# A transformer block of two feed-forwards and a hybrid attention on one core: another order of the seven products and of the filling matmuls

## The chip, the cores and the metric

The kernel runs on one core of a Trainium2 chip. The core has a matrix engine (TensorE, PE in the profile; its weight loads have a row of their own, PEld), VectorE (DVE), ScalarE (ACT), GpSimd (POOL) and SyncE (SP), which issues the DMAs here. The metric is the device time of one execution in microseconds (us); lower is better. Times are the median of several runs.

## The reference

One block in float32, 512 tokens of 1024 features, with a feed-forward on each side of a mixer and a norm at the end:

```
x = x + 0.5 * swiglu(rmsnorm(x, norm_ffn1), w_ffn1_gate, w_ffn1_up, w_ffn1_down)
x = x + hybrid_mixer(rmsnorm(x, norm_mix), w_in, ..., w_out, rel_bias)
x = x + 0.5 * swiglu(rmsnorm(x, norm_ffn2), w_ffn2_gate, w_ffn2_up, w_ffn2_down)
return rmsnorm(x, norm_final)

swiglu(h, w_gate, w_up, w_down) = (silu(h @ w_gate) * (h @ w_up)) @ w_down     # D_FF = 2816
```

The mixer projects to 16 heads of 64 features. Eight of them attend to chosen blocks of keys ("MoBA"). The other eight ("NSA", in two groups of keys) add three results, each with a gate of its own: attention to compressed keys, to selected blocks and to a window. With 512 tokens all blocks are within reach, so that both kinds come down to masked softmax attention with a bias by distance; the compressed keys and values come from a small network of their own. `w_out` projects the heads' outputs back.

## The kernel before, in words

**Three matmuls for one.** A float32 product is made as three products of rounded parts: each operand is split into `hi` (ACT copies it, rounded) and `lo` (DVE or POOL subtracts), and `mm3` (L92 to L95) multiplies hi by hi, hi by lo and lo by hi into one bank of PSUM. These three are called a **triple** here. A triple over 512 tokens has three matmuls of 512 columns, one over half the tokens three of 256.

**Feed-forwards.** A hidden block is 128 of the 2816 hidden features; there are 22. The first six are made plainly (`plain`, 512 columns). The other 16 go two at a time through `pair` (L279): gate and up of two blocks and two halves of the tokens are a 2 x 2 matrix product, made with seven products instead of eight (Strassen and Winograd). A product is 8 triples of 256 columns, 24 matmuls: two halves `m` (gate, up) of four triples over k. The sums of weights S1 to S4 are DVE's (L293), the halves `sph` and `spl` are ACT's and DVE's (L203, L204). The products go into three banks, u, v and w (`pu`, `pv`, `pw`), and some go into a bank that holds an earlier one. What the bank then holds is first copied (`copied`, `wc<-pu`), or else combined with a copy at once (`c11`, `c12`, `c22`, `c21`), before the next product may add to it.

The way down (`down`, L350) has 512-column triples into `pd`, one of two banks of tag `mm`; when an output row block d is complete, DVE adds it to x (`half_added`, L477). The way down of one group of hidden blocks is laid as **fills** between the products of the next group: `mixed` (L382) does it for four hidden blocks at once, that is for two pairs or 28 steps (two to a product). A group has 36 fills at first (six blocks, less twelve that come earlier), then three times 32. By weights, `mixed` puts them behind every second step, with a threefold share behind the last step of the fourth product, S2, which S3 follows into the same bank. So two to five triples stand in a row. `go` (L395) writes PE's order by hand; loads, sums and halves are called 26.0, 12.8 and 8.6 us ahead by the steps' planned costs, and what comes after a product (`then`) is called before the next fill or behind the next step. A scheduler orders the other engines.

**Attention** is a list of steps, each with logits (`ps_s`), a turn (transposes into `ps_t`, then `th` on ACT and `tl` on DVE) and values (`po`). The loop at L1112 takes values of step i - 9, the turn of step i - 6 and logits of step i, with fills between these three. An NSA pair of heads has 13 steps: even head three for each of two kinds, odd head three, then the pair's compressed attention (`cmp_pair`: logits `ps_c` with ten DVE instructions, turn `ps_ct`, values `po<-th,vc`, L1023), then three more. The compressed values come last into the even head's bank; behind them `out_halves` (L869) empties that bank with one instruction of ACT (L882) and two of DVE (L883, L884). Fills are triples of the projections still due (`pp`; DVE's `t`, ACT's and DVE's `xo`, and copies by SP follow when one is complete) and of `w_out` (`pw`). How many stand at a loop step is a table, `share`, in triples; a running target makes whole numbers of it:

```
            if i in busy:
                share[i] += 4.0
            if i + 1 in starts or i + 1 == len(steps):
                share[min(i + 9, len(share) - 1)] += 2.0
```

`busy` holds the steps of `cmp_pair`, `starts` the first step of each head.

Of the kernel before, what the change touches and what calls it, by code (L numbers as in the profile page):

```python
# [32 lines left out]
def block_kernel(ctx: ExitStack, tc: tile.TileContext, A: dict, out: bass.AP):  # L33
# [141 lines left out]
    class Ffn:  # L175
# [103 lines left out]
        def pair(self, f):  # L279
# [8 lines left out]
            def sums(name):  # L288

                a11, a12, a21, a22 = [A[i, j] for i in range(2) for j in range(2)]  # L290
                to, x, y, op = {"S1": (a21, a21, a22, ALU.add), "S2": (a11, a21, a11, ALU.add),
                                "S3": (a21, a11, a22, ALU.subtract), "S4": (a12, a11, a12, ALU.add)}[name]
                nc.vector.tensor_tensor(to, x, y, op)  # L293

            def halves_of(name):
                half[name] = self.split(A[{"A11": (0, 0), "A12": (0, 1), "S1": (1, 0), "S2": (0, 0), "S3": (1, 0),
                                           "S4": (0, 1), "A22": (1, 1)}[name]])

            def run(m, to, a, b, first):
                if first and m == 0:  # L300
                    bank[to] = ps.tile([128, 2, HT], F32, name="p" + to, tag={"u": "s", "v": "t", "w": "o"}[to],
                                       bufs=2)
                hi, lo = half[a]
                for k, x in enumerate(self.moving(b)):
                    mm3(bank[to][:, m], (hi[:, m, k], lo[:, m, k]), x, first and m == k == 0, k == 3, True)
# [29 lines left out]
            for n, (to, a, b, first, then) in enumerate((  # L335
                    ("u", "A11", "B11", True, lambda: copied("u", "u1")),
                    ("v", "A12", "B21", True, c11),
                    ("w", "S1", "T1", True, lambda: copied("w", "w1")),
                    ("u", "S2", "T2", False, lambda: copied("u", "u2")),
                    ("u", "S3", "T3", False, c22),  # L340
                    ("w", "S4", "B22", False, c12),
                    ("u", "A22", "T4", False, c21))):
                for m in range(2):
                    steps.append(Step(1.36, lambda m=m, to=to, a=a, b=b, first=first: run(m, to, a, b, first),
                                      (lambda n=n: loads(n)) if n < 2 and m == 0 else None,
                                      (lambda a=a: sums(a)) if a[0] == "S" and m == 0 else None,
                                      (lambda a=a: halves_of(a)) if m == 0 else None, then if m else None))
# [34 lines left out]
        def mixed(self, steps, fills):  # L382

            out, done = [], 0
            weight = [0 if i < 2 or i == len(steps) - 1 else 3 if i % 14 == 7 else 1 for i in range(len(steps))]
            for i, s in enumerate(steps):
                out.append(s)
                if i % 2 == 0 and i < len(steps) - 1:
                    continue
                upto = sum(weight[:i + 1]) * len(fills) // sum(weight)  # L390
                out += fills[done:upto]
                done = upto
            return out

        def go(self, steps):  # L395
# [4 lines left out]
            late = None  # L400
            with tc.manual_schedule(engines={mybir.EngineType.PE}):
                for i, s in enumerate(steps):
# [5 lines left out]
                    if not s.late and late:  # L408
# [5 lines left out]
                    if s.late:  # L414
# [64 lines left out]
    with ExitStack() as ph:  # L479
# [81 lines left out]
        pairs[18].post.append(put_rows)  # L561
        for i in range(8):
            pairs[26 + 3 * i].post.append(lambda i=i: copied_bias(i))
            pairs[54 + 6 * i].post.append(lambda i=i: copied_cmp(i))
# [3 lines left out]
    with ExitStack() as ph:  # L568
# [529 lines left out]
        for i in range(len(steps)):  # L1098
# [4 lines left out]
            if i + 1 in starts or i + 1 == len(steps):  # L1103
# [187 lines left out]
```

## Time and profile before

| | |
|---|---|
| median of 3 runs | 994.87 us (994.78 to 996.94) |
| the profiled execution's own time | 994.5 us |
| its span, first to last instruction | 992.7 us |
| granted clock of TensorE | 0.999 |
| feed-forward 1, pairs and way down | 75 to 359 us of the span |
| attention's steps | 436 to 620 us |
| feed-forward 2, pairs | 717 to 948 us |

The profile is of one execution. A row of the timeline has the start in us, the duration in us, engine, line, operation, tiles (output <- inputs) with their shapes, and a count; in brackets stands the idle time of the engine before it, and what ended it. Matmuls overlap: the next one starts long before the former one's row ends, so that the pace of PE is read from start to start. `L94` is line 94 of the kernel. Groups show a count, busy us, mean ns of one, and idle us before them with its cause.

### The profile page before, as it was taken

What the parts mean: (1) busy time and instruction counts of PE and PEld (TensorE: products, weight loads), DVE (VectorE), ACT (ScalarE), POOL (GpSimd) and SP (SyncE); (2) the same over time, 40 slices, a digit from 0 to 9 for tenths busy, and PEclk for the clock granted to TensorE, in tenths of its full rate; (3) what the DMA queues carried; (4) which work ended last, traced back from release to release, by engine and by line L of the source; (5) the groups of instructions that cost most, each with busy time, mean ns of one, the idle gap of its engine ahead of it and who ended that gap; (6) DMA issues with size and microseconds to landing.
All of it is one profiled execution on the core that took longest, in us unless ns stands there. A gap on an engine that the chain in (4) does not pass through costs nothing.

```text
span 992.7 us, 15609 instructions
## 1 busy us (share of the span) xinstructions
PE 978.9 (99%) x5944; PEld 867.7 (87%) x5944; DVE 705.4 (71%) x1118; ACT 499.3 (50%) x853; POOL 169.3 (17%) x297
## 2 busy tenths in 40 slices
PE   8999999999999999999999999999999999999997
PEld 6889989999999898888888888888899999999995
DVE  4996675877676475668788885688765778667743
ACT  7654343444444345577666674645443444334444
POOL 0000000000000044256655564800000000000002
PEclk9999999999999999999999999999999999999999
DMA  9633256332320135652323431643333322343002
GB/s 321 225 118 109 84 170 183 119 105 76 116 85 22 54 106 157 211 180 79 92 71 89 120 105 54 195 166 106 106 107 127 103 90 85 107 128 106 23 1 85
DMA packets 45742, 113.86 MB, mean 115 GB/s; under 512 B 10049, under 2 KB 14866, under 8 KB 45668
## 3 DMA queue, kind: packets, MB, share of 16 engines
q1 hardware_dynamic: 45380, 112.73, 36.7%
q8 instruction: 47, 0.77, 0.3%
q14 instruction: 27, 0.22, 0.1%
q10 hardware_dynamic: 288, 0.14, 0.1%
HBM read 100.08 MB, written 5.30 MB: 106 GB/s over the span
## 4 chain that ended last, share of the span: by engine, by line
PE 89%; DVE 2%; DMA 2%; POOL 2%; ACT 2%; SPq 1%; issue 1%; ACTq 0%; DVEq 0%; POOLq 0%
PE pd L93 8%; PE pd L94 8%; PE pd L95 8%; PE pu L95 6%; PE pu L93 6%; PE pu L94 6%; PE pgu L94 4%; PE pgu L95 4%; PE pgu L93 4%; PE pw L95 4%; PE pw L93 4%; PE pw L94 4%; PE ps_t L955 2%; PE pp L93 2%; PE pv L95 2%; PE pp L94 2%
## 5 line engine op out<-in xcount | busy, mean ns | idle before, releaser
L203 ACT ACTIVATE sph<-aw 128x1024 fp32r<-128x1024 f32 x114 | 120.9, 1060 | 229.9 <-PE pu L94 112.1
L204 DVE TENSOR_TENSOR spl<-aw,sph 128x1024 fp32r<-128x1024 f32 x114 | 139.3, 1222 | 56.4 <-ACT sph L203 56.3
L81 ACT ACTIVATE whi<-raw 128x1024 fp32r<-128x1024 f32 (+3 forms) x115 | 112.1, 977 | 103.3 <-PE pgu L94 24.6
L88 DVE TENSOR_TENSOR wlo<-raw,whi 128x1024 fp32r<-128x1024 f32 (+3 forms) x90 | 112.2, 1249 | 30.7 <-ACT whi L81 30.3
L93 PE MATMUL pd<-h,whi 128*128 128x512 f32 x320 | 125.8, 393 | 0.0
L94 PE MATMUL pd<-h,whi 128*128 128x512 f32 x320 | 125.8, 393 | 0.0
L95 PE MATMUL pd<-h,wlo 128*128 128x512 f32 x320 | 124.4, 389 | 0.0
L93 PE MATMUL pu<-th,sph 128*128 128x256 f32 x384 | 108.0, 281 | 0.0
L95 PE MATMUL pu<-th,spl 128*128 128x256 f32 x384 | 107.9, 281 | 0.0
L94 PE MATMUL pu<-tl,sph 128*128 128x256 f32 x384 | 107.8, 281 | 0.0
L293 DVE TENSOR_TENSOR aw<-aw 128x1024 f32<-128x1024 f32 x64 | 78.0, 1219 | 28.8 <-DMA aw<-in_wgu 28.8
L93 PE MATMUL pgu<-xo,whi 128*128 128x512 f32 x192 | 75.2, 391 | 0.9 <-ACT xo L129 0.9
L94 PE MATMUL pgu<-xo,whi 128*128 128x512 f32 x192 | 74.9, 390 | 0.6 <-DVE xo L130 0.6
L94 PEld LDWEIGHTS pu<-tl,sph 128*128 128x128 f32 x384 | 73.5, 191 | 1.8
L95 PE MATMUL pgu<-xo,wlo 128*128 128x512 f32 x192 | 74.7, 389 | 0.0
L93 PEld LDWEIGHTS pu<-th,sph 128*128 128x128 f32 x384 | 72.1, 188 | 2.0
L477 DVE SCALAR_TENSOR_TENSOR x<-pd,x 128x512 f32<-128x512 f32 x72 | 49.4, 687 | 33.7 <-PE pd L95 33.6
L86 POOL TENSOR_TENSOR wlo<-raw,whi 128x128 fp32r<-128x128 f32 x136 | 64.6, 508 | 50.4 <-ACT whi L81 50.4
L95 PEld LDWEIGHTS pu<-th,spl 128*128 128x128 f32 x384 | 72.1, 188 | 0.0
L93 PE MATMUL pw<-xo,sph 128*128 128x256 f32 x256 | 72.0, 281 | 0.0
L95 PE MATMUL pw<-xo,spl 128*128 128x256 f32 x256 | 71.9, 281 | 0.0
L94 PE MATMUL pw<-xo,sph 128*128 128x256 f32 x256 | 71.9, 281 | 0.0
(253 smaller groups left out, 2437.8 us busy)
## 6 DMA issues: line engine op xcount, KB each, us to landing
aw<-in_wgu SPq DMA_DIRECT2D x64, 512.0 KB, 3.8
raw<-in_wgu SPq DMA_DIRECT2D x23, 512.0 KB, 5.5
raw<-in_wd SPq DMA_DIRECT2D x22, 512.0 KB, 3.6
raw<-in_wd2a SPq DMA_DIRECT2D x18, 512.0 KB, 3.8
raw<-in_w_a SPq DMA_DIRECT2D x16, 512.0 KB, 3.7
raw<-in_w SPq DMA_DIRECT2D x8, 512.0 KB, 4.2
kvn<-xo SPq DMA_DIRECT2D x32, 128.0 KB, 2.4
aq<-xo SPq DMA_DIRECT2D x32, 128.0 KB, 2.7
```

The costliest lines, as they stand in the source:

```text
L81: nc.scalar.activation(hi[:, s], src[:, s], AF.Copy)
L86: nc.gpsimd.tensor_tensor(lo[:, i, b], src[:, i, b], f32(hi[:, i, b]), ALU.subtract)
L88: nc.vector.tensor_tensor(lo[:, s], src[:, s], f32(hi[:, s]), ALU.subtract)
L93: nc.tensor.matmul(p, w[0], v[0], start=first, stop=False, skip_group_check=again)
L94: nc.tensor.matmul(p, w[0], v[1], start=False, stop=False, skip_group_check=again)
L95: nc.tensor.matmul(p, w[1], v[0], start=False, stop=last, skip_group_check=again)
L203: nc.scalar.activation(hi, v, AF.Copy)
L204: nc.vector.tensor_tensor(lo, v, f32(hi), ALU.subtract)
L293: nc.vector.tensor_tensor(to, x, y, op)
L477: nc.vector.scalar_tensor_tensor(xs[d], p, 0.5, xs[d], ALU.mult, ALU.add)
L955: nc.tensor.transpose(p[:, wide:wide + 128], lps[qi][:, j * 128:(j + 1) * 128], ident)
```

## The change

**In both feed-forwards.** The seven products keep their operands and banks but stand in another order: u A11, v A12, **u S2, w S1**, u S3, w S4, u A22. No two products into one bank follow each other in it. The four sums are made two at a time, S1 and S2 ahead of S2's product, S4 and S3 ahead of S3's, and S3 is written over A11's place instead of A21's. A step is now half of what it was (two triples of k, planned at 0.67 and 0.69 us), so a group has 56 steps. `mixed` puts exactly one fill behind a chosen step: behind the second half-steps from the sixth step on, and, as there are more fills than those 25 places, behind evenly chosen first half-steps. No fill is left over behind a group. `go` tells a first half-step by its cost, and doesn't call a former product's `then` for a fill that stands inside a product. The steps at which the bias rows are written and copied have their numbers doubled.

**In attention** the two triples that stood at the ninth step behind the end of an even NSA head's own steps now stand at the ninth step behind `cmp_pair`'s, that is at the loop step of its values. Everything else in the table stays.

```diff
@@ -289,19 +289,21 @@
 
                 a11, a12, a21, a22 = [A[i, j] for i in range(2) for j in range(2)]
                 to, x, y, op = {"S1": (a21, a21, a22, ALU.add), "S2": (a11, a21, a11, ALU.add),
-                                "S3": (a21, a11, a22, ALU.subtract), "S4": (a12, a11, a12, ALU.add)}[name]
+                                "S3": (a11, a11, a22, ALU.subtract), "S4": (a12, a11, a12, ALU.add)}[name]
                 nc.vector.tensor_tensor(to, x, y, op)
 
+            two_sums = {"S2": ("S1", "S2"), "S3": ("S4", "S3")}
+
             def halves_of(name):
-                half[name] = self.split(A[{"A11": (0, 0), "A12": (0, 1), "S1": (1, 0), "S2": (0, 0), "S3": (1, 0),
+                half[name] = self.split(A[{"A11": (0, 0), "A12": (0, 1), "S1": (1, 0), "S2": (0, 0), "S3": (0, 0),
                                            "S4": (0, 1), "A22": (1, 1)}[name]])
 
-            def run(m, to, a, b, first):
-                if first and m == 0:
+            def run(m, n, to, a, b, first):
+                if first and m == n == 0:
                     bank[to] = ps.tile([128, 2, HT], F32, name="p" + to, tag={"u": "s", "v": "t", "w": "o"}[to],
                                        bufs=2)
                 hi, lo = half[a]
-                for k, x in enumerate(self.moving(b)):
+                for k, x in list(enumerate(self.moving(b)))[2 * n:2 * n + 2]:
                     mm3(bank[to][:, m], (hi[:, m, k], lo[:, m, k]), x, first and m == k == 0, k == 3, True)
 
             def copied(to, name):
@@ -335,16 +337,19 @@
             for n, (to, a, b, first, then) in enumerate((
                     ("u", "A11", "B11", True, lambda: copied("u", "u1")),
                     ("v", "A12", "B21", True, c11),
+                    ("u", "S2", "T2", False, lambda: copied("u", "u2")),
                     ("w", "S1", "T1", True, lambda: copied("w", "w1")),
-                    ("u", "S2", "T2", False, lambda: copied("u", "u2")),
                     ("u", "S3", "T3", False, c22),
                     ("w", "S4", "B22", False, c12),
                     ("u", "A22", "T4", False, c21))):
                 for m in range(2):
-                    steps.append(Step(1.36, lambda m=m, to=to, a=a, b=b, first=first: run(m, to, a, b, first),
-                                      (lambda n=n: loads(n)) if n < 2 and m == 0 else None,
-                                      (lambda a=a: sums(a)) if a[0] == "S" and m == 0 else None,
-                                      (lambda a=a: halves_of(a)) if m == 0 else None, then if m else None))
+                    for at in range(2):
+                        begins = m == at == 0
+                        steps.append(Step(
+                            (0.67, 0.69)[at], lambda m=m, at=at, to=to, a=a, b=b, first=first: run(m, at, to, a, b, first),
+                            (lambda n=n: loads(n)) if n < 2 and begins else None,
+                            (lambda a=a: [sums(s) for s in two_sums[a]]) if a in two_sums and begins else None,
+                            (lambda a=a: halves_of(a)) if begins else None, then if m == at == 1 else None))
             return steps
 
         def down(self, w, fs, then, tag="mm", group=1):
@@ -382,22 +387,22 @@
         def mixed(self, steps, fills):
 
             out, done = [], 0
-            weight = [0 if i < 2 or i == len(steps) - 1 else 3 if i % 14 == 7 else 1 for i in range(len(steps))]
+            ends, inner = range(5, len(steps) - 1, 2), range(6, len(steps) - 2, 2)
+            more = max(0, len(fills) - len(ends))
+            taken = set(ends[:len(fills)]) | {inner[(2 * n + 1) * len(inner) // (2 * more)] for n in range(more)}
             for i, s in enumerate(steps):
                 out.append(s)
-                if i % 2 == 0 and i < len(steps) - 1:
-                    continue
-                upto = sum(weight[:i + 1]) * len(fills) // sum(weight)
-                out += fills[done:upto]
-                done = upto
-            return out
+                if i in taken:
+                    out.append(fills[done])
+                    done += 1
+            return out + fills[done:]
 
         def go(self, steps):
 
             start, at = [0.0], [0, 0, 0]
             for s in steps:
                 start.append(start[-1] + s.cost)
-            late = None
+            late, inside = None, False
             with tc.manual_schedule(engines={mybir.EngineType.PE}):
                 for i, s in enumerate(steps):
                     for j, ahead in enumerate((26.0, 12.8, 8.6)):
@@ -405,13 +410,16 @@
                             if steps[at[j]].ahead[j]:
                                 steps[at[j]].ahead[j]()
                             at[j] += 1
-                    if not s.late and late:
+                    if not s.late and late and not inside:
                         late()
                         late = None
                     s.run()
                     for post in s.post:
                         post()
-                    if s.late:
+                    if s.cost < 0.68:
+                        inside = True
+                    elif s.late:
+                        inside = False
                         if late:
                             late()
                         late = s.then
@@ -558,10 +566,10 @@
                 fills = ffn.down(A["wd1"][f:], fs, half_added)
             else:
                 steps += ffn.down(A["wd1"][f:], fs, then, None, 4)
-        pairs[18].post.append(put_rows)
+        pairs[36].post.append(put_rows)
         for i in range(8):
-            pairs[26 + 3 * i].post.append(lambda i=i: copied_bias(i))
-            pairs[54 + 6 * i].post.append(lambda i=i: copied_cmp(i))
+            pairs[52 + 6 * i].post.append(lambda i=i: copied_bias(i))
+            pairs[108 + 12 * i].post.append(lambda i=i: copied_cmp(i))
         ffn.go(steps)
 
 
@@ -1100,7 +1108,10 @@
                 share[i] += 0.5
             if i in busy:
                 share[i] += 4.0
-            if i + 1 in starts or i + 1 == len(steps):
+                share[i + 9] += 2.0
+            elif starts.get(i + 1) in (9, 11, 13, 15):
+                continue
+            elif i + 1 in starts or i + 1 == len(steps):
                 share[min(i + 9, len(share) - 1)] += 2.0
             if starts.get(i) in (0, 2, 4):
                 share[i + 1] += 3.0
```

What becomes of it in the order of PE, first pair of feed-forward 1, between product A12 (`pv`) and the one behind it, before:

```order
L95 MATMUL pv_842<-xo_740,spl_776 128x256
L93 MATMUL pd_880<-h_410,whi_722 128x512
L94 MATMUL pd_880<-h_411,whi_722 128x512
L95 MATMUL pd_880<-h_410,wlo_723 128x512
L93 MATMUL pd_880<-h_461,whi_722 128x512
L94 MATMUL pd_880<-h_462,whi_722 128x512
L95 MATMUL pd_880<-h_461,wlo_723 128x512
L93 MATMUL pw_887<-xo_353,sph_801 128x256
```

After, inside product A12 (its m = 1):

```order
L95 MATMUL pv_842<-xo_740,spl_777 128x256
L93 MATMUL pd_863<-h_410,whi_722 128x512
L94 MATMUL pd_863<-h_411,whi_722 128x512
L95 MATMUL pd_863<-h_410,wlo_723 128x512
L93 MATMUL pv_842<-xo_355,sph_776 128x256
```

and behind the same product:

```order
L95 MATMUL pv_842<-xo_740,spl_777 128x256
L93 MATMUL pd_863<-h_461,whi_722 128x512
L94 MATMUL pd_863<-h_462,whi_722 128x512
L95 MATMUL pd_863<-h_461,wlo_723 128x512
L93 MATMUL pu_813<-th3_129,sph_801 128x256
L94 MATMUL pu_813<-tl3_130,sph_801 128x256
```

The two triples that stood in a row behind A12 are now one in the middle of its second half and one behind it, and S2 into `pu` follows it in place of S1 into `pw`. Over the whole of feed-forward 1 the order has 51 runs of fills before the final way down, now 132 (33 runs of two triples, 10 of three, 6 of four and 2 of five, and two triples more ahead of the final way down; now 132 of one). In feed-forward 2 it is 52 (one more run of two), now 132. The final way down of feed-forward 1 has 34 triples in a row with those two, now 32. Behind the last product of feed-forward 2 stand the 32 transposes `px` in one piece, where 13 of them stood ahead of its fifth product before.

PE in attention, where the second NSA pair's compressed values end its even head (`po_4804`), before:

```order
L926 MATMUL ps_s_5078<-kvn_3964,aq_4743 128x384
L1023 MATMUL po_4804<-th_5000,vc_4431 128x512
L1023 MATMUL po_4989<-th_5000,vc_4431 128x512
L955 MATMUL ps_t_5096<-ident_84,lpn_4903 128x128
L955 MATMUL ps_t_5096<-ident_84,lp_4927 128x128 x2
L93 MATMUL pp_5062<-xo_3361,whi_4640 128x512
L94 MATMUL pp_5062<-xo_3362,whi_4640 128x512
L95 MATMUL pp_5062<-xo_3361,wlo_4641 128x512
L925 MATMUL ps_s_5107<-kvn_3962,aq_4743 128x512
```

and after:

```order
L934 MATMUL ps_s_5042<-kvn_3964,aq_4743 128x384
L1031 MATMUL po_4804<-th_4994,vc_4431 128x512
L1031 MATMUL po_4983<-th_4994,vc_4431 128x512
L93 MATMUL pp_4837<-xo_3467,whi_4440 128x512
L94 MATMUL pp_4837<-xo_3468,whi_4440 128x512
L95 MATMUL pp_4837<-xo_3467,wlo_4441 128x512
L963 MATMUL ps_t_5063<-ident_84,lpn_4903 128x128
L963 MATMUL ps_t_5063<-ident_84,lp_4927 128x128 x2
L93 MATMUL pp_5100<-xo_3352,whi_4689 128x512
L94 MATMUL pp_5100<-xo_3353,whi_4689 128x512
L95 MATMUL pp_5100<-xo_3352,wlo_4690 128x512
L933 MATMUL ps_s_5104<-kvn_3962,aq_4743 128x512
```

One triple now stands between the values and the transposes and another behind the transposes. At the loop steps that are four earlier two triples less stand; the order of the three other pairs changes in the same way.

DVE there: the rows that belong to the end of a filling projection (`t<-pp`, `xo<-t`) stood among those of the steps ahead of the head's end. Before:

```order
L601 TENSOR_TENSOR t_5033<-pp_4837,R_100 128x512
L933 ISA lp_5004,m_4953<-ps_s_5003,tb_4740 128x512
L933 ISA m_4953 128x1
L1016 TENSOR_TENSOR th_5000<-ps_ct_4995,th_5000 64x512
L613 TENSOR_TENSOR xo_3508<-t_5033,xo_3507 128x512
L933 ISA lpn_5023,m_5028<-ps_s_5022,tb_4740 128x128
L933 ISA m_5028 128x1
L933 ISA lpn_5023,m_5028<-ps_s_5022,tb_4740 128x256
```

They now stand behind it, `t` behind the first of `out_halves`' two instructions (`to`) and `xo` four rows behind the second (`o51`):

```order
L891 TENSOR_TENSOR to_5056<-po_4804,o50_5054 64x512
L609 TENSOR_TENSOR t_5071<-pp_4837,R_100 128x512
L967 TENSOR_TENSOR tl_5013<-ps_t_5007,th_5012 128x512
L892 TENSOR_TENSOR o51_5055<-to_5056,po_4804 64x512
L948 RECIPROCAL m_5022<-m_5022 128x3
L941 ISA lp_5105,m_5022<-ps_s_5104,tb_4740 128x512
L941 ISA m_5022 128x1
L967 TENSOR_TENSOR tl_5068<-ps_t_5063,th_5067 128x384
L621 TENSOR_TENSOR xo_3508<-t_5071,xo_3507 128x512
```

## The prediction

> **What bounds the kernel.** I read the page first, then busy time by stage, then TensorE's (PE's) rows in order of time inside two stages.
>
> ```profile
> span 992.7 us, 15609 instructions
> PE 978.9 (99%) x5944; PEld 867.7 (87%) x5944; DVE 705.4 (71%) x1118; ACT 499.3 (50%) x853; POOL 169.3 (17%) x297
> ...
> 75.00:359.00 284.00, 284.00 (x1895) 260.82 (x1895) 195.82 (x222) 118.90 (x158) 8.84 (x9) 1.00 0.33 102
> 436.00:620.00 184.00, 180.35 (x1048) 153.47 (x1047) 144.09 (x415) 124.22 (x323) 108.35 (x219) 1.00 0.34 91
> 717.00:948.00 231.00, 231.00 (x1604) 215.24 (x1603) 161.92 (x181) 98.22 (x126) 0.00 (x0) 1.00 0.31 96
> ```
>
> Behind a stretch stand its length, the busy time of PE, weight loads, DVE, ACT and POOL, and the granted clock, DMA share and GB/s. PE is never idle in the two feed-forward stretches (284.00 of 284.00, 231.00 of 231.00), at a granted clock of 1.00. So nothing that another engine does sooner can shorten these; only the pace of PE's own instructions can. In attention (436 to 620) PE lacks 3.65 us. A busy PE can still go slower or faster, so I take the pace from start to start:
>
> ```profile
> 300.61 0.40 PE L93 MATMUL pd<-h,whi 128*128 128x512 f32 x1
> ...
> 301.99 0.28 PE L93 MATMUL pu<-xo,sph 128*128 128x256 f32 x1
> ...
> 304.00 0.28 PE L95 MATMUL pu<-xo,spl 128*128 128x256 f32 x1
> ```
>
> From 301.99 to 304.00 there are 17 steps between 256-wide matmuls: 0.118 us each. The two triples before them took 1.38 us.
>
> **FFNs: the pace of a triple.** The matmuls are the same in number and shape; only their neighbours change. So the term is what it costs PE to enter a run of 512-wide matmuls out of 256-wide ones:
>
> ```profile
> 96.62 0.40 PE L93 MATMUL pd<-h,whi 128*128 128x512 f32 x1
> ...
> 97.32 0.40 PE L93 MATMUL pd<-h,whi 128*128 128x512 f32 x1
> ...
> 100.05 0.28 PE L93 MATMUL pu<-th,sph 128*128 128x256 f32 x1
> ...
> 332.14 0.40 PE L93 MATMUL pd<-h,whi 128*128 128x512 f32 x1
> ...
> 355.29 0.39 PE L93 MATMUL pp<-xo,whi 128*128 128x512 f32 x1
> ```
>
> The last two rows bracket the final way down, 34 triples in a row: 23.15 / 34 = 0.681 us each. The run of five from 96.62 to 100.05 took 3.43, which is 0.025 more than 5 x 0.681. The first triple of the run took 0.70 (96.62 to 97.32); with rows that are rounded to 0.01 I take 0.697, so that 0.016 of the 0.025 falls on it and the rest on the second. A single triple between 256-wide matmuls stands in attention:
>
> ```profile
> 490.02 0.39 PE L93 MATMUL pp<-xo,whi 128*128 128x512 f32 x1
> ...
> 490.72 0.28 PE L99 MATMUL po<-th,kvn 128*128 128x256 f32 x1
> ```
>
> It took 0.70 as well. By the built programs' order, FFN 1 has 51 runs of two to five triples before the final one, and 132 single triples after; FFN 2 has 52 and 132. Each FFN therefore goes from about 51 x 0.025 = 1.3 us of entries to 132 x 0.016 = 2.1 us: **+0.8 each, +1.7 for both** with rounding upwards. Its bounds: nothing, if a single triple enters free; and 264 x 0.025 less 103 x 0.025, or +4.0, if a single one pays the whole entry.
>
> The Trainium skill (TensorE: Matmul & The Clock Gate, Back-to-back issue gap) gives a warm matmul N / 2.4 + 2.5 ns whatever stood before it, 216 ns for 512 columns and 109 for 256. By that rule the FFN term is zero; the rows here differ from it, with 0.681 / 3 = 0.227 us in a long run, more at its beginning, and 0.118.
>
> **FFNs: the other order.** What the new order takes away is the follow-up of two products into one bank: S3 went into bank u right after S2, whose copy ACT makes (the row `wc<-pu`).
>
> ```profile
> 285.81 0.28 PE L95 MATMUL pu<-th,spl 128*128 128x256 f32 x1
> ...
> 286.98 0.58 ACT L309 ACTIVATE wc<-pu 128x512 f32<-128x512 f32 x1
> ...
> 288.67 0.28 PE L93 MATMUL pu<-th,sph 128*128 128x256 f32 x1
> ```
>
> S2's last matmul starts at 285.81, the copy ends at 287.56 and S3 begins at 288.67: 1.1 us to spare, with four triples in between. So the old order cost no wait here and the new one saves none. Its cover is larger: the whole S1 product (24 x 0.118 = 2.8 us) plus its fills lies between S2 and S3, so I cost it at nothing. Without any cover it would cost the 1.75 from 285.81 to 287.56, in 16 pairs. DVE's four sums of a pair (S1 to S4) are now made two and two instead of one by one, at most one sum earlier or later than before, and planned 12.8 us ahead of their use; the loads belong to the same two products as before, so SP's queue has the same order there. The way down's bank is needed again soonest at one place of the first group: with 12 x 0.118 + 0.70 = 2.1 us of PE's work between the last triple of one output and the next triple into its bank, where it was 24 x 0.118 + 0.70 = 3.5. DVE's addition has to fit into that behind whatever DVE is at; I cost it at nothing, and at some tenths, once in each FFN, if it comes late.
>
> **Attention: where PE waits.** Here PE's idle time sits on the transposes:
>
> ```profile
> L955 PE MATMUL ps_t<-ident,lpn 128*128 128x128 f32 x144 | 27.8, 275 | 2.9 <-DVE tl L959 2.9
> ```
>
> Its five waits are these, each with the row that PE issued before it:
>
> ```profile
> 464.30 0.40 PE L95 MATMUL pp<-xo,wlo 128*128 128x512 f32 x1
> 464.86 0.30 PE L955 MATMUL ps_t<-ident,lpn 128*128 128x128 f32 x1 [0.16 <-DVE tl L959]
> ...
> 491.82 0.62 PE L1023 MATMUL po<-th,vc 128*128 128x512 f32 x2
> 493.74 0.30 PE L955 MATMUL ps_t<-ident,lpn 128*128 128x128 f32 x1 [1.29 <-DVE tl L959]
> ...
> 521.05 0.63 PE L1023 MATMUL po<-th,vc 128*128 128x512 f32 x2
> 522.58 0.30 PE L955 MATMUL ps_t<-ident,lpn 128*128 128x128 f32 x1 [0.90 <-DVE tl L959]
> ...
> 525.62 0.34 PE L100 MATMUL po<-tl,kvn 128*128 128x384 f32 x1
> 526.28 0.41 PE L955 MATMUL ps_t<-ident,lpn 128*128 128x128 f32 x2 [0.32 <-DVE tl L959]
> ...
> 552.53 0.40 PE L95 MATMUL pp<-xo,wlo 128*128 128x512 f32 x1
> 553.12 0.30 PE L955 MATMUL ps_t<-ident,lpn 128*128 128x128 f32 x1 [0.19 <-DVE tl L959]
> ```
>
> All five come at `po<-th,vc`, or one or two steps behind it, the compressed values that finish a pair's even head: the four places to which the change moves its two triples. Start to start, less 0.23 per 512-wide matmul (0.175 for 384): 0.33, 1.46, 1.07, 0.49, 0.36, together 3.7 us. The chain behind the longest one, on DVE and ACT:
>
> ```profile
> 486.34 0.56 DVE L933 CUSTOM_DVE_ANT_0 lpn<-ps_s,tb 128x384 f32<-128x384 f32 x1 [1.22 <-PE ps_s L926]
> ...
> 488.07 0.69 DVE L601 TENSOR_TENSOR t<-pp,R 128x512 f32<-128x512 f32 x1 [0.21 <-PE pp L95]
> ...
> 490.53 0.87 DVE L613 TENSOR_TENSOR xo<-t,xo 128x512 fp32r<-128x512 f32 x1
> ...
> 493.03 0.56 DVE L959 TENSOR_TENSOR tl<-ps_t,th 128x384 fp32r<-128x384 f32 x1 [0.34 <-ACT th L958]
> ...
> 487.83 1.06 ACT L81 ACTIVATE whi<-raw 128x1024 fp32r<-128x1024 f32 x1 [0.19 <-PE pp L94]
> ...
> 489.28 0.61 ACT L612 ACTIVATE xo<-t 128x512 fp32r<-128x512 f32 x1
> ```
>
> Before the head's end DVE still waits for PE (1.22 at 486.34), and has 0.34 of idle time left between `xo` at 490.53 and `tl` at 493.03; `xo` (0.87) stands in its way, and ACT has `whi` and `xo` in its. In the new order two triples less stand before, so DVE gets its scores sooner, and the fill's `t` and `xo` come behind `tl` in DVE's row. A triple (0.70) also stands between the values and the transposes. The weights and the copies that SP sends for a job (its queue is in order) move with the triples by the same two, and the heads that need them come later; I cost that at nothing. So 1.46 loses 0.70 to the triple and 0.87 to DVE: gone. 1.07 goes the same way. Of 0.49 I count half, since `t` (0.69) now stands before that `tl`, against 1.4 us of PE work. Of 0.33 and 0.36 I count half. Sum 1.46 + 1.07 + 0.25 + 0.35 = 3.1; I take off 0.2 for new tenths where the triples left: **-2.9**. What is late next is PE itself, since each triple moved is 0.70 of its own work. Bounds: all 3.7 gone; or nothing gained and the removed cover missed at its old place. No wait stands there now, so the nearest price is the longest of the five, and +1.5 is the other end.
>
> **Sum.** +1.7 - 2.9 = -1.2. The profiled execution took 994.5 us (span 992.7 and 1.8 around it), so 993.3; the median of the runs is 994.87, 0.4 above, so **993.7**.
>
> **Rivals.**
> - *PE leaves the slow pace of the 256-wide matmuls.* Once they go faster, behind transposes near the end:
>
> ```profile
> 949.70 0.28 PE L95 MATMUL pu<-th,spl 128*128 128x256 f32 x1
> ...
> 951.85 0.40 PE L93 MATMUL pd<-h,whi 128*128 128x512 f32 x1
> ```
>
>   19 steps in 2.15 us, 0.113 each. If a single triple leaves PE in that state, 2,688 products gain 0.0045 each, 12 us: about 982. Against it: after runs of two as of five the pace was 0.118 at once. 6%.
> - *The entry is free*: a matmul's pace doesn't depend on what stood before it. Then -2.9 alone, 992.0. Against it stand the 0.70 rows; for it, that they are only 0.016 above a long run's. 10%. This is what the formula of the Trainium skill above would give.
> - *Slower: every switch between widths costs more than the entry that I counted*, since the change also cuts products in the middle. The FFNs get 264 - 103 = 161 more interruptions. With the upper bound, 0.025 each, and no gain in attention the time is 994.9 + 4.0 = 998.9. It decides for slower from (3.0 + 2.9) / 161 = 0.037 us per interruption with attention's gain, or 0.019 without it. For it: 0.70 against 0.681 shows that PE settles only after some matmuls, and a product cut in two has to settle more often. 12%.
> - *The attention wait only moves*, because DVE has hardly a pause ahead of the head's end (0.34 behind `xo`) and behind it gets `t` and `xo` there: +1.7 alone, 996.6. 17%.
> - *The change does not do what it says*: the order shows single triples and the moved fills, so 0.
>
> **How the numbers follow.** The forecast as summed has 55%. A measurement of this kernel tells about 0.3% (3 us) from no change. Same: the forecast mostly, the moved wait, most of the free entry; 0.67. Faster: the fast pace, part of the free entry, the forecast's end where all 3.7 go and the FFN term is small; 0.19. Slower: 0.14. The range reaches from -3.7 with no entry cost (about 991.0) to most of the upper bounds (997.3); the two ends beyond, 982 and 998.9, are left out.
>
> **What would show it.** Triples in the FFNs at 0.69 to 0.70 start to start and 256-wide matmuls still at 0.118 would confirm the FFN term; 0.113 would make the forecast too high by up to 12 us, and a first matmul behind a triple well over 0.118 too low. In attention the idle time of `ps_t` should fall from 2.9 to under 1 us; new waits at the steps that lost their triples, or one step later on the same `tl`, would show that it only moved. Any idle time of PE inside the FFNs would refute that the new order is covered.

## The result, and the profile after

The changed kernel took **983.82 us** (median of 5 runs, 982.56 to 986.12) where the one before took 994.87: a ratio of 0.9888 with an interval of 0.9869 to 0.9906, or 9.4 to 13.0 us less. The forecast was 993.7, within 991.0 and 997.3. The direction was right, the size was not: the time lies near the 982 us of a rival that had been given 6%.

The page of the changed kernel, its first line and its line on the engines:

```profile
span 981.0 us, 15636 instructions
PE 970.0 (99%) x5944; PEld 857.6 (87%) x5944; DVE 702.2 (72%) x1118; ACT 499.0 (51%) x853; POOL 168.9 (17%) x297
```

As many matmuls, PE just as busy by its share, and a span 11.7 us shorter: PE's busy time fell by 8.9 us, since it worked faster, and its idle time by 2.8. Busy time by stretch says where. The kernel before, from the first product to the last matmul of the final way down in feed-forward 1, in attention (first logits to last values), and from feed-forward 2's first product to the end (columns as in the prediction):

```profile
82.54:355.06 272.52, 272.52 (x1842) 251.21 (x1841) 185.92 (x211) 111.69 (x147) 5.47 (x5) 1.00 0.34 103
433.30:614.40 181.10, 177.54 (x1039) 151.57 (x1038) 143.37 (x418) 124.05 (x320) 109.34 (x221) 1.00 0.34 92
710.89:992.70 281.81, 275.22 (x1869) 254.03 (x1867) 183.76 (x216) 120.27 (x169) 5.18 (x4) 1.00 0.28 88
```

and the same three in the changed kernel:

```profile
82.39:350.42 268.03, 268.03 (x1843) 245.47 (x1841) 185.03 (x211) 111.73 (x147) 5.48 (x5) 1.00 0.34 104
428.02:607.03 179.01, 176.75 (x1040) 151.78 (x1038) 142.67 (x418) 123.82 (x320) 109.35 (x222) 1.00 0.34 93
703.66:981.00 277.34, 270.72 (x1869) 248.45 (x1867) 182.86 (x216) 120.14 (x169) 5.18 (x4) 0.99 0.28 90
```

Feed-forward 1 lost 4.49 us and feed-forward 2 lost 4.47, PE without a pause in the first both times and at the same clock. Attention lost 2.09. The rest of the 11.7 is 0.64 between feed-forward 1 and attention, where one wait is gone, and small shifts.

PE's rows in the first pair after show the moment at which the pace changes. Ahead of the first fill, and behind it:

```profile
85.93 0.28 PE L93 MATMUL pv<-xo,sph 128*128 128x256 f32 x1
...
86.63 0.40 PE L93 MATMUL pd<-h,whi 128*128 128x512 f32 x1
...
87.33 0.28 PE L93 MATMUL pv<-xo,sph 128*128 128x256 f32 x1
...
88.58 0.28 PE L95 MATMUL pv<-xo,spl 128*128 128x256 f32 x1
```

From 85.93 to 86.63 there are 6 steps of 0.117 us, the pace of before. The triple takes 0.70. From 87.33 to 88.58 there are 11 steps of **0.1136** each, on the same engine, with the same operands, and that pace stays to the end of the stretch. So one triple put PE into the faster pace that the prediction had seen near the end of the kernel before.

In attention the groups of transposes and of compressed logits:

```profile
L963 PE MATMUL ps_t<-ident,lpn 128*128 128x128 f32 x144 | 27.9, 275 | 0.8 <-DVE tl L967 0.8
L1000 PE MATMUL ps_c<-kc,aq 128*128 128x64 f32 x32 | 4.1, 273 | 1.1 <-DVE t L611 1.0
```

The idle time of `ps_t` fell from 2.9 to 0.8 us, as forecast; 1.1 now stands at `ps_c`, behind DVE's `t` of a fill.

### The profile page after: what moved, and what is told of

It is laid out like the page before. It is cut to its first block, busy times and chain, and to the rows that moved or that the text cites. A ratio compares the mean times of both kernels' runs of the same rounds, so it can differ in the third digit from the quotient of the medians.

```text
span 981.0 us, 15636 instructions
## 1 busy us (share of the span) xinstructions
PE 970.0 (99%) x5944; PEld 857.6 (87%) x5944; DVE 702.2 (72%) x1118; ACT 499.0 (51%) x853; POOL 168.9 (17%) x297
## 4 chain that ended last, share of the span: by engine, by line
PE 93%; DMA 2%; POOL 1%; DVE 1%; issue 1%; SPq 1%; ACT 0%; DVEq 0%; ACTq 0%; POOLq 0%
PE pd L94 8%; PE pd L95 8%; PE pd L93 8%; PE pu L93 6%; PE pu L95 6%; PE pu L94 6%; PE pw L93 4%; PE pw L95 4%; PE pw L94 4%; PE pgu L94 4%; PE pgu L95 4%; PE pgu L93 4%; PE pv L93 3%; PE pv L95 3%; PE pv L94 3%; PE pp L93 3%
## 5 line engine op out<-in xcount | busy, mean ns | idle before, releaser
L95 PEld LDWEIGHTS pd<-h,wlo 128*128 128x128 f32 x320 | 60.1, 188 | 13.4
L93 PE MATMUL pw<-xo,sph 128*128 128x256 f32 x256 | 70.7, 276 | 0.0
L94 PE MATMUL pw<-xo,sph 128*128 128x256 f32 x256 | 70.7, 276 | 0.0
```

Source lines behind the costliest of these rows:

```text
L93: nc.tensor.matmul(p, w[0], v[0], start=first, stop=False, skip_group_check=again)
L94: nc.tensor.matmul(p, w[0], v[1], start=False, stop=False, skip_group_check=again)
L95: nc.tensor.matmul(p, w[1], v[0], start=False, stop=last, skip_group_check=again)
```

## The experiments

Eleven kernels and the changed one once more, each measured beside "before" on the same chip. "Stretch" below means feed-forward 1 from its first product to the last matmul of the final way down, and feed-forward 2 from its first product to the end: 272.52 and 281.81 us before, 268.03 and 277.34 after.

**The two parts alone.** The changed feed-forwards with the old table of attention, and the reverse:

```diff
-                share[i + 9] += 2.0
-            elif starts.get(i + 1) in (9, 11, 13, 15):
-                continue
-            elif i + 1 in starts or i + 1 == len(steps):
+            if i + 1 in starts or i + 1 == len(steps):
```

> The feed-forwards of after with the attention table of before. Read from the two traces, the feed-forwards' stretches are 4.5 us shorter each and attention 2.1 us. Theory (the parts are independent, the pace of the 256-wide matmuls pays for all of the feed-forwards): 994.9 - 9.0 = 985.9 us, pace 0.1133 from start to start in both. Rival (part of the gain comes from what attention leaves behind): 987 or more.

Measured: 986.59 us, ratio 0.9910 (0.9890 to 0.9931), about 9.0 us less; stretches 268.03 and 277.34, to 0.01 us those of after.

> The feed-forwards of before with the attention table of after. Theory (the moved fill is worth what the attention stretch shows): 994.9 - 2.1 = 992.8 us, transposes' idle time 2.9 down to about 1 us, a new wait of some 1.0 us at one ps_c. Rival (attention only got shorter because its inputs came earlier or PE was in another pace): 994.9 us. 256-wide matmuls stay at 0.118 in both feed-forwards.

Measured: 993.42 us, ratio 0.9977 (0.9966 to 0.9989), 1.1 to 3.4 us less; stretches 272.52 and 281.82, those of before. In its profile, of the slowest of its executions (995.76 us), the waits on `tl` at the compressed values are 0.33 to 0.37, as in after's, and the new wait at `ps_c` is 0.32; the whole group of `ps_t` still shows 2.8, not the expected 1, because PE waited 0.9 for POOL's `lpn` and 0.9 for another `tl` early in the attention. By the times, the parts add up, and the feed-forwards are four fifths of the whole.

**The order of the products, or the single fills?** After, with the products and their sums in the order of before:

```diff
...
-                    ("u", "S2", "T2", False, lambda: copied("u", "u2")),
                     ("w", "S1", "T1", True, lambda: copied("w", "w1")),
+                    ("u", "S2", "T2", False, lambda: copied("u", "u2")),
...
```

> After, but with the seven products (and the sums) in the order of before; fills stay single, at the same places. Theory A (the length of the run of 512-wide matmuls decides the pace): 0.113 us for 256-wide matmuls, as in after; S3 follows S2 into one bank with one triple between, so PE waits for the copy 1.75 - 0.70 = 1.05 us in each of 16 pairs: 983.8 + 16.8 = 1000.6 us. Theory B (the new order of the products makes the pace): 0.118 us, 1000.6 + 11.5 = 1012 us.

Measured: 1000.94 us, ratio 1.0059 (1.0041 to 1.0077). PE's rows at the first S3:

```profile
98.95 0.39 PE L95 MATMUL pd<-h,wlo 128*128 128x512 f32 x1
100.16 0.39 PE L93 MATMUL pu<-th,sph 128*128 128x256 f32 x1 [0.82 <-ACT wc L311]
```

ACT's row there, and then the group of these matmuls:

```profile
99.53 0.58 ACT L311 ACTIVATE wc<-pu 128x512 f32<-128x512 f32 x1
...
L93 PE MATMUL pu<-th,sph 128*128 128x256 f32 x384 | 107.8, 281 | 12.8 <-ACT wc L311 12.8
```

S3 starts when ACT's copy ends (100.11). From the last matmul ahead to S3 there are 1.21 us where 0.23 would do: 1.0 or a little more in 15 of the 16 pairs (in the last one, transposes stand between S2 and S3), and the first step of S3 then takes 0.22 where 0.113 is usual. The stretches are 277.12 and 285.70, 17.45 together above after's. But for the first five steps behind such a wait the 256-wide matmuls stay at 0.1133. So theory A: the order of the products doesn't make the pace. It makes room for the copy, without which single fills cost more than they bring.

**Two fills in a row, new order.**

```diff
...
+            n = (len(fills) + 1) // 2
+            taken = {ends[(2 * j + 1) * len(ends) // (2 * n)] for j in range(n)}
...
-                    out.append(fills[done])
-                    done += 1
+                    out += fills[done:done + 2]
+                    done += 2
...
```

> After, but with two fills in a row at half as many places (the ends of second half-steps), the products in the new order. Theory A (a run of one triple leaves PE in the fast pace, a run of two in the slow one): 256-wide matmuls at 0.118, 983.8 + 11.5 us for the pace, less 2 x (132 x 0.020 - 66 x 0.027) = 1.7 us of entries: 993.6 us. Theory B (the order of the products, or where the fills stand, decides): 0.113 stays, 983.8 - 1.7 = 982.1 us.

Measured: 994.33 us, ratio 0.9987 (0.9973 to 1.0001); nearly all of the gain is gone, near the 993.6 of theory A. Behind a run of two triples:

```profile
101.00 0.40 PE L93 MATMUL pd<-h,whi 128*128 128x512 f32 x1
...
101.69 0.28 PE L93 MATMUL pu<-th,sph 128*128 128x256 f32 x1
...
102.98 0.28 PE L95 MATMUL pu<-th,spl 128*128 128x256 f32 x1
```

Eleven steps in 1.29 us, 0.117 each, the slow pace at once. Stretches 273.22 and 282.27, slightly above those of before.

**From which length on?** Fills cut into single 512-wide matmuls, in runs of 1 to 9 in shuffled order:

```diff
...
+            ones = [(f, j) for f in fills for j in range(3)]
...
+                cycle = list(range(1, 10))
+                self.rng.shuffle(cycle)
+                sizes += cycle
...
```

> After, but the fills are cut into single 512-wide matmuls and laid in runs of 1 to 9 of them, in shuffled order, all at the ends of second half-steps, in both feed-forwards. Theory A1 (up to a whole triple leaves PE in the fast pace, from some length between 4 and 6 on it is left in the slow one, whatever the pace before): 256-wide matmuls stand at 0.113 behind runs of 3 and at 0.118 behind runs of 6 to 9, each in both orders; runs of 1 and 2 either make the pace 0.113 or leave it as it was. Theory A2 (what counts is that the run is one accumulation triple hi-hi, hi-lo, lo-hi, not its length): runs of 3 that are cut across triples fall out, as do 1 and 2. Theory A3 (only the state before counts and a long run resets it: three matmuls toggle the pace): 0.113 and 0.118 alternate.

One execution: 999.02 us, at a mean clock of 0.993, with two long pauses of PE inside runs; only its rows are used. Behind a run of four, then of three, and of five matmuls (rows with x2 hold two):

```profile
105.09 0.28 PE L93 MATMUL pw<-xo,sph 128*128 128x256 f32 x1
...
106.38 0.28 PE L95 MATMUL pw<-xo,spl 128*128 128x256 f32 x1
106.50 0.63 PE L374 MATMUL pd<-h,whi 128*128 128x512 f32 x2
106.97 0.40 PE L374 MATMUL pd<-h,wlo 128*128 128x512 f32 x1
107.20 0.28 PE L93 MATMUL pw<-xo,sph 128*128 128x256 f32 x1
...
107.99 0.28 PE L94 MATMUL pw<-xo,sph 128*128 128x256 f32 x1
...
181.50 0.28 PE L93 MATMUL pw<-xo,sph 128*128 128x256 f32 x1
...
182.40 0.28 PE L95 MATMUL pw<-xo,spl 128*128 128x256 f32 x1
```

After four: 11 steps in 1.29 (0.117). After three: 7 in 0.79 (0.113). After five, from the fourth matmul on: 8 in 0.90 (0.1125 from rounded rows). Over both feed-forwards, all runs of PE's rows that no wait disturbed, by the mean pace of the fifth to tenth 256-wide matmul behind each:

| 512-wide matmuls in a row | 1 | 2 | 3 | 4 | 5 | 6 | 7 | 8 | 9 |
|---|---|---|---|---|---|---|---|---|---|
| cases | 17 | 17 | 18 | 17 | 18 | 20 | 16 | 14 | 17 |
| pace behind, us | 0.113 | 0.113 | 0.113 | 0.118 | 0.113 | 0.118 | 0.118 | 0.118 | 0.118 |

No case differs from the others in its column, whether the pace ahead had been 0.113 or 0.118, and whichever matmul of a triple the run began with. A2 and A3 fall. A1 holds but for its one threshold: five is fast, though four is not. So in these feed-forwards PE's pace has two states, and the length of the last run of 512-wide matmuls sets which.

**All fills narrow.** The way down in 256-wide matmuls:

```diff
...
+                for s in (slice(0, HT), slice(HT, S)):
+                    mm3(bank[d][:, s], w, (v[0][:, s], v[1][:, s]), k == s.start == 0, k == n - 1, True)
...
```

> After, but every fill except one in each group of hidden blocks is made as six 256-wide matmuls (both halves of its 512 columns) in place of three 512-wide ones; the one that stays 512-wide is the second of its group. Theory (256-wide matmuls hold the pace of 0.1133 that a single triple sets, and the 0.020 us that each single triple pays above 0.680 goes): 256 x 0.020 = 5.1 us less than after, 983.8 - 5.1 = 978.7 us, six narrow ones at 0.680. Rival 1 (without single triples between them the 256-wide matmuls fall back to 0.118): up to 256 x 6 x 0.0045 + 11.5 = 18 us more, about 1002 us. Rival 2 (twice the weight loads, 256 x 3 = 768 more, cost something of their own): the six at more than 0.70, slower than 983.8 us.

Measured: 999.95 us, ratio 1.0047 (1.0030 to 1.0065). Behind the one 512-wide fill, then a narrow one, then a product:

```profile
89.74 0.28 PE L93 MATMUL pu<-th,sph 128*128 128x256 f32 x1
...
90.42 0.28 PE L93 MATMUL pd<-h,whi 128*128 128x256 f32 x1
...
91.14 0.28 PE L93 MATMUL pu<-th,sph 128*128 128x256 f32 x1
...
91.72 0.28 PE L95 MATMUL pu<-th,spl 128*128 128x256 f32 x1
```

Six steps in 0.68 (0.113), six narrow ones in 0.72 (0.120), then five in 0.58 (0.116 to 0.118). The time is near the 1002 of rival 1, and the sign of rival 2 is there too: six narrow matmuls took 0.72, over its 0.70 and over six at the slow pace. The narrow fill itself ends the fast pace. What in it does so was not found; their additional weight loads were not tested apart. It isn't the change of bank alone: in the next kernel products of 256-wide matmuls follow each other in different banks at 0.1133 (there `pu` ends and `pv` begins in the middle of such a stretch).

**Long runs with a single triple behind.** If the last run alone sets the state, a long run may stand, as long as a single triple follows soon:

```diff
...
+                taken[i], taken[i + 1] = n - 1, 1
...
```

> After, with the fills of each group laid as runs of seven triples behind second half-steps, each followed by one single triple behind the next half-step (six 256-wide matmuls later). Theory (a long run leaves the slow pace, the next single triple ends it): per eight triples 0.027 of entry for the long run, 6 x 0.0045 = 0.027 of slow pace and 0.020 for the single triple, 0.074 us in place of 8 x 0.020 = 0.160. Over eight groups of 32 to 36 triples that is 33 x 0.086 = 2.8 us less: 983.8 - 2.8 = 981.0 us. Rival (the slow pace stays until the end of a product or longer, as in e4_doubles): 994. Rival 2 (runs of 4.8 us without a product starve PE afterwards, waits on sph or aw): over 984 us.

Measured: 983.77 us, ratio 0.9895 (0.9882 to 0.9909): the time of after, not the 981.0 of the theory. PE's rows in the first group, at a wait in a run and then behind another run:

```profile
105.04 0.39 PE L95 MATMUL pd<-h,wlo 128*128 128x512 f32 x1
105.92 0.50 PE L93 MATMUL pd<-h,whi 128*128 128x512 f32 x1 [0.49 <-DVE x L490]
...
120.42 0.28 PE L93 MATMUL pu<-xo,sph 128*128 128x256 f32 x1
...
121.12 0.40 PE L93 MATMUL pd<-h,whi 128*128 128x512 f32 x1
...
121.82 0.28 PE L93 MATMUL pu<-xo,sph 128*128 128x256 f32 x1
...
122.39 0.28 PE L95 MATMUL pu<-xo,spl 128*128 128x256 f32 x1
```

Behind the long run 6 steps in 0.70 (0.117), behind the single triple 5 in 0.57 (0.114). That is the theory's mechanism, and the rival of 994 falls. But the stretches are only 0.49 and 0.46 shorter than after's, since a wait of 0.65 for a bank of the way down came up in each.

Then runs of fifteen and one:

> The same with runs of fifteen triples and one: 0.074 us per sixteen triples in place of 0.320; 16 x 0.246 + 2 of the remainders, about 4.0 us less than after: 979.8 us. Rival 2 (10 us of PE's work without a product, so that the weights of the way down come late or the products' engines pause): waits inside the feed-forwards, over 984 us.

Measured: 989.11 us, ratio 0.9947 (0.9934 to 0.9961): over rival 2's 984, and with a wait inside the feed-forwards. PE's rows in a run of fifteen, and DVE's there:

```profile
170.64 0.80 PE L93 MATMUL pd<-h,whi 128*128 128x512 f32 x1 [5.35 <-DVE x L490]
171.23 0.63 PE L94 MATMUL pd<-h,whi 128*128 128x512 f32 x1
...
174.64 0.63 PE L93 MATMUL pd<-h,whi 128*128 128x512 f32 x1
...
168.75 1.23 DVE L293 TENSOR_TENSOR aw<-aw 128x1024 f32<-128x1024 f32 x1 [8.00 <-DMA aw<-in_wgu]
169.90 1.28 DVE L490 SCALAR_TENSOR_TENSOR x<-pd,x 128x512 f32<-128x512 f32 x2
```

PE waited 5.35 us for a bank of the way down. The addition (`x<-pd,x`) that frees it stood on DVE behind a sum of weights, and that one waited 8.00 us for the load of `aw`. So it was the products' own weights that came late, not those of the way down. Behind the wait PE went at half its pace: from 171.23 to 174.64 the 8 steps take 0.426 each, at a granted clock of 0.51 (170.6 to 175.4).

Runs of seven and one in the later groups alone, and the changed kernel on the same chip:

> After, with its single fills in the first group of each feed-forward, where runs of seven made PE wait 0.65 us for a bank of the way down, and runs of seven triples and one in the other three groups. Theory (0.086 us less per eight triples and no wait): 24 x 0.086 = 2.1 us less than after in the same call. Rival (the lumps take as much in other places, as in e7_seven_and_one, whose whole time was that of after): no difference.

> The changed kernel itself, on the same chip as e11_lumps_later: 983.8 us, with the attention waits as in after.

Measured: 981.86 us (980.96 to 984.78) with runs only in the later groups, 982.08 (981.57 to 983.99) for the changed kernel itself. The stretches were 266.99 and 276.32, so 1.04 and 1.02 shorter: the 2.1 us are there. The whole time shows no difference between the two: runs of one kernel spread by 2 to 4 us here. The version is not shown to beat the changed kernel.

**Attention.** The two triples of each NSA pair at both places, then at neither:

> After, with two fill triples of each NSA pair at both places, the old one and the one behind the compressed values. Theory A (DVE's t and xo of a filling projection stand in the way of the turn's tl; the moved triples are cover too, about half and half): the waits on tl at the compressed values, 3.7 us before and 1.4 after, are 2 to 2.8 here. Theory B (the triple behind the values is cover, and nothing else counts): 1.4 as in after.

Measured: 986.37 us, ratio 0.9916 (0.9903 to 0.9930). The steps on `tl` at the compressed values, start to start less PE's own pace as in the prediction, are 0.33, 0.33, 0.34 and 0.72, together 1.7: nearer B's 1.4 than A's 2 to 2.8.

> After, with these two triples at neither place (they come later, in the rest of the loop). Theory A: the waits on tl at the compressed values come back to about half, 2 to 2.8 us. Theory B: to all of it, 3.7 us or more, and the time is about 2.3 us above after: 986 us.

Measured: 989.33 us, ratio 0.9947 (0.9933 to 0.9962). The waits on `tl` at the compressed values: 0.36, 0.67 (at a `po`), 1.03, 1.03 and 0.36, together 3.5, where before (with the 0.24 of a `po` that the prediction didn't count) they were 3.9. B had asked for 3.7 or more, A for 2 to 2.8. A further 0.41 stands two loop steps ahead of the third pair's values. The second pair with neither, on PE and then on DVE:

```profile
485.28 0.64 PE L1031 MATMUL po<-th,vc 128*128 128x512 f32 x2
486.77 0.30 PE L963 MATMUL ps_t<-ident,lpn 128*128 128x128 f32 x1 [0.86 <-DVE tl L967]
...
485.58 0.56 DVE L941 CUSTOM_DVE_ANT_0 lpn<-ps_s,tb 128x384 f32<-128x384 f32 x1 [1.05 <-POOL lp L954]
```

and PE there with both:

```profile
491.17 0.39 PE L95 MATMUL pp<-xo,wlo 128*128 128x512 f32 x1
491.73 0.30 PE L963 MATMUL ps_t<-ident,lpn 128*128 128x128 f32 x1 [0.18 <-DVE tl L967]
```

With neither, `xo` stands no longer in DVE's way (DVE is idle for 1.05 ahead of `lpn`), and PE still waits 1.03. With both it waits 0.33, the 1.03 less one triple of 0.70. So theory B, nearly: the triple between the values and the transposes is cover, and that is what pays. The whole times of these two lie above after's, and in both profiles PE waited elsewhere too: with both, 1.4 us on POOL's `lpn` at the start of the attention and 1.6 at the `pw` near its end; with neither, on `m` (2.0 us by the group of `ps_t`). That the number of triples elsewhere in the loop made these waits was not tested.

## Why the prediction was wrong

**The FFN term failed, in its first sentence**: "the term is what it costs PE to enter a run of 512-wide matmuls". It left out what a run does to the 256-wide matmuls behind it. They run at 0.1178 behind two or more triples and at 0.1133 behind one. Summed over PE's rows, the steps from all 2,688 take 5.77 us less in feed-forward 1 and 5.80 less in feed-forward 2, 11.6 together, though the 36 ahead of each first fill keep the old pace. The rival had the mechanism and the price (2,688 x 0.0045 = 12) but was put at 6%. The reason against it, "after runs of two as of five the pace was 0.118 at once", was no evidence, since it speaks of lengths two to five alone: the feed-forwards of before hold no run of one, and the change makes nothing else. The stretch from 949.70 to 951.85, where the fast pace stood in the same trace, should have weighed more, and the range should have reached what it would give. It wasn't the only one either, though the prediction says "once". In feed-forward 1 of before, behind the six matmuls of `pb` that make the bias, stand these rows:

```profile
126.73 0.28 PE L95 MATMUL pw<-xo,spl 128*128 128x256 f32 x1
...
127.42 0.28 PE L95 MATMUL pw<-xo,spl 128*128 128x256 f32 x1
```

The six steps between them take 0.680 by the rows in ns, 0.1133 each.

**The entry was mis-sized.** I took 0.697 for a single triple and so 0.016 above a long run's pace, 0.025 for a longer run. The triples of after stand 0.700 apart from what follows (132 of 132 in feed-forward 1, by PE's rows in ns), 0.020 above, and a longer run pays 0.027. Then 264 x 0.020 - 103 x 0.027 = +2.5, not +1.7. With -11.6 that is -9.1, and the two stretches show -4.49 and -4.47.

**The other order** was costed at nothing with its cover, and this was right: no wait appears in the feed-forwards after, and the price without the cover, "the 1.75 from 285.81 to 287.56", shows in the kernel with the old order: 1.75 less one triple is 1.05, and PE waited 1.0 at most places.

**Attention** was forecast at -2.9 and gave -2.09 by its stretch, 1.1 to 3.4 us when alone. The chain was right and the split of it was not: "1.46 loses 0.70 to the triple and 0.87 to DVE". The triple did its 0.70, while DVE's part is the step from 1.46 to the 1.03 with neither, 0.4 in this pair, and from 1.07 to 1.03, nothing, in the next. PE's rows after, where the second pair ends and where new idle time stands:

```profile
485.58 0.39 PE L95 MATMUL pp<-xo,wlo 128*128 128x512 f32 x1
486.14 0.30 PE L963 MATMUL ps_t<-ident,lpn 128*128 128x128 f32 x1 [0.18 <-DVE tl L967]
...
498.91 0.30 PE L1000 MATMUL ps_c<-kc,aq 128*128 128x64 f32 x1 [1.01 <-DVE t L611]
```

0.33 to 0.37 is left in each pair, 1.4 in all: 2.3 less than the 3.7 counted before. The new 1.01 at `ps_c`, 0.46 in the second profile of the same kernel, is the `t` of a fill that now comes late; the 0.2 taken off "for new tenths" was too little for it.

Of what would show it, the triples at 0.70, `ps_t` under 1 us and no idle time in the feed-forwards came as written. The pace of 0.113 was named as that which would make the forecast too high "by up to 12 us", and it did.

## What to carry to other kernels

On a stretch where PE never waits, read the pace of its matmuls from start to start in each shape, and look for a second value of it anywhere in the trace: a difference of 4% in a pace that holds for thousands of instructions outweighs every wait. When a change makes a neighbourhood that the trace doesn't contain (here a run of one), runs of two to five say nothing of it; give the other state a chance to match. A trick that needs room, such as single fills, is worth what its cover costs: try it with the old order too, to see which part pays.

## What the runs showed that I had not expected

- **Two paces of PE at one granted clock.** A 256-wide matmul takes 0.1133 or 0.1178 us, and the number of 512-wide matmuls of the way down in the last run sets which: 0.1133 behind 1, 2, 3 and 5, 0.1178 behind 4 and 6 to 9, in 154 of 154 runs. Other neighbours set it too. In the kernel before, 13 transposes of 128 columns left the quicker pace, and so did the six matmuls of `pb`, two of 384 columns and four of 512; the narrow fills left the slower one. So the length of a run is not the whole rule. Why five differs from four stays open, and what in PE holds the state; the last step of a run is 0.229 to 0.237 us where 0.113 follows and 0.225 to 0.230 where 0.118 does, so it doesn't tell them apart. The Trainium skill (TensorE: Matmul & The Clock Gate, Back-to-back issue gap) gives N / 2.4 + 2.5 ns as the gap of an isolated matmul, which would be an estimated 109 ns for 256 columns, and says that in a stream the weight loads set the spacing too. Even the quicker pace is 4 ns above that estimate, and the formula has no second one; no run here tells the share of the weight loads.
- **The feed-forwards repeat to 0.01 us** from run to run (268.03 and 277.34 in the kernels that share them), so their stretches settle a tenth where the whole time spreads by 2 to 4 us. Part of the spread is made elsewhere, where PE waits for GpSimd and afterwards goes at half its pace. PE's rows at such a place, between attention and feed-forward 2 in the kernel with long runs in the later groups:

```profile
637.58 1.05 PE L151 MATMUL pr<-ones_f,acc 128*128 128x1 f32 x8 [0.96 <-POOL acc L145]
...
638.81 0.62 PE L94 MATMUL pgu<-xo,whi 128*128 128x512 f32 x1
...
642.22 0.40 PE L93 MATMUL pgu<-xo,whi 128*128 128x512 f32 x1
```

  Eight 512-wide steps from 638.81 to 642.22 take 0.426 each, where 0.227 is usual, and then the pace is back; the granted clock from 638.5 to 642.3 is 0.55. A wait of 1.0 us and eight tiny matmuls were thus followed by a loss of 8 x 0.2 = 1.6 us besides. The Trainium skill (same page, the HAM clock gate) gives 426.7 ns for a 512-wide matmul at half clock, which agrees; it puts the drop behind an idle window of about 3.4 us, while here PE had had some 2 us with little work.
